# A 1 KB copy from input to output, issued on ScalarE's DMA ring at the start of a DMA-bound running logsumexp

## The chip, the cores and the metric

The kernel runs on one core of one Trainium2 chip. The metric is the device time of one execution in microseconds (us). Profiled runs also have a span, which is about 1.8 us shorter than the time.

## The reference, cut to what matters

```python
def setup_inputs():
    B, S, D = (4, 4096, 4128)
    return {'x': np.random.randn(B, S, D).astype(np.float32)}

def reference(x):
    ...
    out[:, 0, :] = x[:, 0, :].copy()
    for t in range(1, S):
        mx = np.maximum(out[:, t - 1, :], x[:, t, :])
        out[:, t, :] = mx + np.log(np.exp(out[:, t - 1, :] - mx) + np.exp(x[:, t, :] - mx))
```

It is a running logsumexp along S: 270.5 MB are read and 270.5 MB written, each once.

## The kernel before

The 4096 rows of each of four batches are cut into steps of 128 x 3 rows (and one of 128 x 2 per batch), 44 steps in all. A step is loaded into one of four buffers, goes through Exp (ScalarE), sums (VectorE, with TensorE for the sum over partitions) and Ln (ScalarE) in place, and is stored from the same buffer. SyncE issues every load and every store, in program order:

```python
    nc.scalar.preload_act_table_set("natural_log_exp_and_others")
    ...
        def load(self):
            full = xpool.tile([P, R, D], FP32, name="xt")
            self.xt = full[:, :self.r, :]
            nc.sync.dma_start(out=self.xt, in_=self.dram(x))

        def store(self):
            nc.sync.dma_start(out=self.dram(out), in_=self.xt)
    ...
    ahead = bufs - 1                 # bufs is 4
    for s in steps[:bufs]:
        s.load()
    stored = 0

    def result(k):
        nonlocal stored
        k.act(ACT.Ln)
        if k.c == lastc:
            k.t.store()
            if bufs <= stored + ahead < len(steps):
                steps[stored + ahead].load()
            stored += 1
```

The softmax here doesn't subtract the row's maximum and nothing guards it: scores larger than these inputs give would overflow.

Of the kernel before, what the change touches and what calls it, by code (L numbers as in the profile page):

```python
# [38 lines left out]
def kernel(  # L39
# [14 lines left out]
    nc = tc.nc  # L54
# [5 lines left out]
    order = [NC - 1] + list(range(NC - 1))  # L60
    firstc, lastc = order[0], order[-1]

    nc.scalar.preload_act_table_set("natural_log_exp_and_others")  # L63
    consts = ctx.enter_context(tc.tile_pool(name="consts", bufs=1))
    excl, rest, pick = _constants(nc, consts)
# [178 lines left out]
```

## Time and profile before

| | before |
|---|---|
| time, median of 6 runs | 1266.37 us (1263.28 to 1266.55) |
| span of the profiled run | 1262.5 us |
| ring of all loads and stores (q1) | 99.4% of 16 DMA engines' span |
| VectorE, ScalarE busy | 81%, 73% |
| HBM traffic | 270.53 MB read, 270.53 MB written |

The prediction shows the main lines: the sixteen DMA engines are full nearly throughout, so the bytes set the time. Two views of SyncE are added here, because the experiments turn on them. First its timeline of the first 70 us (columns: start, duration, engine, line, operation, tiles, count):

```profile
0.80 1.94 SPq L103 DMA_DIRECT2D xt<-in_x_dram  x4
41.31 22.79 SPq L106 DMA_DIRECT2D out_dram<-xt  x2
67.86 0.34 SPq L103 DMA_DIRECT2D xt<-in_x_dram  x1
```

The second row is two stores merged: one issued at 41.31 us, the other done being issued at 41.31 + 22.79 = 64.10 us. The fifth load follows at 67.86 us.

### The profile page before, as it was taken

How to read it: one execution, taken by the hardware profiler on the slowest of the kernel's cores; microseconds unless marked ns; L12 is line 12 of the kernel's file. 1: busy time of each engine (PE TensorE's matmuls, PEld its weight loads, DVE VectorE, ACT ScalarE, POOL GpSimd, SP SyncE). 2: the span in 40 equal slices, each digit the busy share in tenths (PEclk: the TensorE clock that was granted, in tenths of full speed). 3: DMA queues.
4: the chain of work that ended last, by engine and by line, in shares of the span. 5: the costliest groups of instructions: out<-in, count | busy, mean ns of one | idle time of the engine just before them, and what ended most of it. 6: DMA issues, size and time to landing. Idle time of an engine off the chain costs nothing.

```text
span 1262.5 us, 3545 instructions
## 1 busy us (share of the span) xinstructions
PE 480.5 (38%) x876; PEld 220.3 (17%) x876; DVE 1024.4 (81%) x858; ACT 921.0 (73%) x353; POOL 1.5 (0%) x10
## 2 busy tenths in 40 slices
PE   2445433333334434443324434443432443444332
PEld 1212111111111112211111112111111211111111
DVE  4999878888888888888679888887867988887784
ACT  4986677777777776668669776666966977666784
POOL 0000000000000000000000000000000000000000
PEclk9865555565555555556556565656555656555656
DMA  9999999999999999999999999999999999999997
GB/s 410 410 444 431 426 433 438 432 430 435 436 427 430 443 432 429 435 437 432 433 435 429 429 441 432 428 437 435 424 425 431 434 433 432 430 436 433 433 409 340
DMA packets 12692, 541.29 MB, mean 429 GB/s; under 512 B 1408, under 2 KB 1408, under 8 KB 1408
## 3 DMA queue, kind: packets, MB, share of 16 engines
q1 hardware_dynamic: 12672, 541.07, 99.4%
q8 instruction: 7, 0.11, 0.0%
q14 instruction: 13, 0.11, 0.0%
HBM read 270.53 MB, written 270.53 MB: 429 GB/s over the span
## 4 chain that ended last, share of the span: by engine, by line
DMA 69%; ACT 19%; issue 7%; DVE 3%; SPq 0%; PE 0%; DVEq 0%; ACTq 0%
DMA xt<-in_x_dram 63%; ACT xt L118 19%; DMA out_dram<-xt 6%; DVE xt L86 3%; DVE tot L86 1%; SPq L106 0%; PE above L83 0%; DVE carry L155 0%; DVEq L239 0%; ACTq L118 0%; DVE carry_t L155 0%; DVEq L86 0%
## 5 line engine op out<-in xcount | busy, mean ns | idle before, releaser
L118 ACT ACTIVATE xt<-xt 128x3072 f32<-128x3072 f32 (+3 forms) x352 | 919.7, 2692 | 328.8 <-DMA xt<-in_x_dram 315.0
L83 PE MATMUL above<-tot,excl 128*128 128x512 f32 (+1 forms) x396 | 255.1, 714 | 476.9 <-DVE tot L86 472.6
L86 DVE TENSOR_TENSOR xt<-xt,above 128x2048 f32<-128x2048 f32 (+3 forms) x220 | 393.4, 1788 | 0.0
L86 DVE TENSOR_TENSOR xt<-xt 128x1024 f32<-128x1024 f32 (+1 forms) x160 | 197.0, 1231 | 179.9 <-ACT xt L118 177.5
L86 DVE TENSOR_TENSOR tot<-xt 128x1024 fp32r<-128x1024 f32 (+1 forms) x176 | 217.1, 1234 | 40.4 <-ACT xt L118 18.9
L86 DVE TENSOR_TENSOR xt<-tot,above 128x1024 f32<-128x1024 f32 (+1 forms) x220 | 221.5, 1007 | 0.0
L83 PEld LDWEIGHTS above<-tot,excl 128*128 128x128 f32 x396 | 104.4, 305 | 607.4 <-DVE tot L86 566.9
L83 PE MATMUL above<-tot,rest 128*128 128x512 f32 x240 | 129.2, 633 | 205.1 <-DVE xt L86 205.1
L83 PE MATMUL above<-carry,pick 128*128 128x512 f32 x160 | 139.5, 972 | 0.0
L83 PEld LDWEIGHTS above<-tot,rest 128*128 128x128 f32 x240 | 53.1, 276 | 295.9 <-DVE xt L86 294.1
L83 PE MATMUL above<-carry_t,pick 128*128 128x32 f32 x80 | 25.2, 409 | 83.2 <-DVE xt L86 83.2
L83 PEld LDWEIGHTS above<-carry,pick 128*128 128x128 f32 x160 | 51.5, 322 | 11.1
L83 PEld LDWEIGHTS above<-carry_t,pick 128*128 128x128 f32 x80 | 20.2, 311 | 110.3 <-DVE xt L86 108.3
L155 DVE COPY carry<-xt 32x1024 f32<-32x1024 f32 x40 | 27.6, 691 | 1.4
L155 DVE COPY carry_t<-xt 32x32 f32<-32x32 f32 x40 | 7.1, 178 | 1.4
L63 ACT ACT_TABLE_LOAD x1 | 1.3, 1283 | 0.8 <-PEq L228 0.8
L77 DVE MEMSET carry<- 128x1024 f32 x1 | 0.9, 912 | 1.1 <-PEq L228 1.1
L24 POOL TENSOR_SCALAR_AFFINE_SELECT rest<-rest 128x128 fp32r<-128x128 f32 x1 | 0.3, 293 | 0.0
L24 POOL TENSOR_SCALAR_AFFINE_SELECT pick<-pick 128x128 f32<-128x128 f32 x1 | 0.3, 292 | 0.1
L24 POOL TENSOR_SCALAR_AFFINE_SELECT excl<-excl 128x128 fp32r<-128x128 f32 x1 | 0.3, 292 | 0.0
L23 POOL MEMSET excl<- 128x128 f32 x1 | 0.2, 204 | 0.3 <-POOLq L228 0.3
L23 POOL MEMSET rest<- 128x128 f32 x1 | 0.2, 204 | 0.0
(6 smaller groups left out, 0.7 us busy)
## 6 DMA issues: line engine op xcount, KB each, us to landing
xt<-in_x_dram SPq DMA_DIRECT2D x40, 6192.0 KB, 41.9
out_dram<-xt SPq DMA_DIRECT2D x40, 6192.0 KB, 27.7
xt<-in_x_dram SPq DMA_DIRECT2D x4, 4128.0 KB, 37.0
out_dram<-xt SPq DMA_DIRECT2D x4, 4128.0 KB, 25.4
```

Source lines behind the costliest of these rows:

```text
L23: nc.gpsimd.memset(t.bitcast(FP32), 1.0 - fill)
L24: nc.gpsimd.affine_select(out=t, in_=t, pattern=[[step, P]], compare_op=op, fill=fill, base=base, channel_multiplier=-step if step else 1,)
L63: nc.scalar.preload_act_table_set("natural_log_exp_and_others")
L77: nc.vector.memset(carry, 0.0)
L83: nc.tensor.matmul(o, lhsT=w, rhs=rhs, start=start, stop=True, skip_group_check=True)
L86: nc.vector.tensor_tensor(out=o, in0=a, in1=b, op=mybir.AluOpType.add)
L118: nc.scalar.activation(v, v, func)
L155: nc.vector.tensor_copy(cr[96:, :], t.xt[96:, n, a:b])
```

## The change

One line: before anything else, ScalarE copies 16 rows of 16 words from the input to the output. The rows are overwritten by the first store, so the result does not change. The likely intent is to see whether a second, otherwise unused ring costs or gives anything while the loads begin.

```diff
     firstc, lastc = order[0], order[-1]
 
+
+    nc.scalar.dma_start(out=out[0, :16, :16], in_=x[0, :16, :16])
     nc.scalar.preload_act_table_set("natural_log_exp_and_others")
```

The built programs differ by this one instruction on ScalarE, and by a wait: the first store waits for the copy as well.

## The prediction

> **What bounds the kernel now.** I read the page first: the busy shares, the slices, the DMA queues.
>
> ```profile
> PE 480.5 (38%) x876; PEld 220.3 (17%) x876; DVE 1024.4 (81%) x858; ACT 921.0 (73%) x353; POOL 1.5 (0%) x10
> ...
> DMA  9999999999999999999999999999999999999997
> ...
> q1 hardware_dynamic: 12672, 541.07, 99.4%
> q8 instruction: 7, 0.11, 0.0%
> q14 instruction: 13, 0.11, 0.0%
> ...
> xt<-in_x_dram SPq DMA_DIRECT2D x40, 6192.0 KB, 41.9
> out_dram<-xt SPq DMA_DIRECT2D x40, 6192.0 KB, 27.7
> ```
>
> No compute engine is above 81%, while the sixteen DMA engines are full in 39 of 40 slices. All 88 transfers go through one ring, q1, the one that SyncE issues on. Its packets fill 99.4% of the span of sixteen engines: 0.994 x 1262.5 = 1254.9 us for the mean engine. So only about 7.6 us of the span is not transfer. The packet records of the trace say the same from below: a row of three (49,536 bytes on one partition) has a median of 1829 ns and a row of two 1222 ns, and each engine carries 8 partitions of each of 80 large and 8 small transfers, 640 x 1.829 + 64 x 1.222 = 1248.8 us. Whatever keeps sizes and counts as they are cannot end much before that.
>
> Where the 7.6 us lie is read from the busy time by stretch (columns: stretch, length, busy us and count of each engine, granted clock, DMA share, GB/s):
>
> ```profile
> 0.00:15.00 15.00, 0.00 (x0) 0.00 (x0) 0.95 (x2) 3.17 (x3) 1.52 (x10) 1.00 0.94 387
> ...
> 60.00:120.00 60.00, 26.11 (x51) 12.39 (x51) 58.63 (x52) 51.72 (x20) 0.00 (x0) 0.59 1.00 432
> 120.00:240.00 120.00, 48.48 (x88) 22.48 (x88) 100.44 (x84) 86.00 (x32) 0.00 (x0) 0.56 1.00 432
> ...
> 600.00:1000.00 400.00, 148.25 (x273) 67.44 (x271) 322.12 (x272) 290.19 (x114) 0.00 (x0) 0.56 1.00 432
> ...
> 1220.00:1240.00 20.00, 7.65 (x16) 3.69 (x14) 14.40 (x14) 15.40 (x8) 0.00 (x0) 0.59 0.87 375
> 1240.00:1255.00 15.00, 4.52 (x8) 1.83 (x8) 8.47 (x8) 6.92 (x4) 0.00 (x0) 0.73 0.70 301
> ```
>
> The middle is full (share 1.00, 432 GB/s). What is lost lies at the start (0.06 x 15 = 0.9 us) and after 1220 us (0.13 x 20 + 0.30 x 15 = 7.1 us), where the last steps are computed with little left to load. The reader is to take two things from this: a delay of the first load moves the whole full stretch, so it comes out at the end one for one; and a delay on a compute engine early on costs nothing while the ring still has transfers queued.
>
> Last I read the timeline of the first 15 us and the waits, because the change sits there:
>
> ```profile
> 0.80 1.28 ACT L63 ACT_TABLE_LOAD   x1 [0.80 <-PEq L228]
> ...
> 0.80 1.94 SPq L103 DMA_DIRECT2D xt<-in_x_dram  x4
> ...
> 13.12 7.36 ACT L118 ACTIVATE xt<-xt 128x2112 f32<-128x2112 f32 x4 [11.04 <-DMA xt<-in_x_dram]
> ```
>
> SyncE issues four loads from 0.80 to 2.74 us, about 0.49 us each. ScalarE loads its table by 2.08 us and then stands idle for 11.04 us until the first load lands at 13.09 us. The first store is issued only at 41.31 us.
>
> **What the Trainium skill says.** (1) "DMA: Bandwidth & Descriptors", section "Issuing engines are not separate DMA queues": transfers begun by ScalarE and by SyncE end up on the same sixteen engines and interleave there; a second issuer saves only issue time. So the copy opens no further bandwidth. The trace before cannot confirm it, having one data ring. (2) The same page, "Queues, rings and completion order": an engine alternates between the rings that have work, at packet boundaries. Here a packet of the load lasts 1.2 us (step of two rows) or 1.8 us, so a copy that comes behind one waits at most about that long per engine; the trace shows a like case, instruction fetches (q8, q14) taken between the packets of q1. (3) The same page, "Specifications": below 512 bytes a write is a read-modify-write. The copy's rows are 64 bytes, so it is inefficient, but there are sixteen. (4) "ScalarE: Activation LUTs", "What ACT_TABLE_LOAD costs": about 1283 ns for the table load itself. The trace agrees to the digit (row of L63: 1 time, 1283 ns).
>
> **The change, part by part.** Removed: nothing. Moved: nothing; the comparison of instruction order shows ScalarE with one row more, a copy of 16x16 ahead of the table load, and the same rows on SyncE and GpSimd. On PE and VectorE only tile numbers differ. Each later transfer takes the next of the eight completion semaphores in rotation, the same rotation one place on, so no wait gets a new partner. One wait is new: the first store overwrites the rows the copy wrote, so it waits for the copy too.
>
> Issue on ScalarE: one issue like SyncE's, about 0.49 us (1.94 / 4), perhaps less with 16 rows for 128. The table load then ends at 2.08 + 0.49 = 2.6 us instead of 2.08; the first Exp starts at 13.12 on the landing. Slack 11.04 us, use 0.49: **cost 0**.
>
> New wait of the first store: the copy must have landed by 41.31 us. It is issued at about 0.8 us. Even behind a whole packet of the load on every engine (1.2 us) and with some us of latency (the first load's data begins to move about 1 us after its issue in the packet records, 1.8 us into the span), it is down before 6 us: **cost 0**.
>
> Bytes: 16 x 64 = 1 KB written and 1 KB read. At 429 GB/s that is 2.4 ns, beside 541 MB: **cost 0** as bandwidth. As packets it is one data packet more on each engine at most, where it now handles 704. The cost is thus a fixed time: an instruction fetch of 8 KB takes 0.31 us in mid-kernel in the packet records; I estimate 0.1 to 0.5 us for a read of 64 bytes and a small write, if nothing of it overlaps the load's packets.
>
> The first load's issue: both issuers start at about 0.80 us. If they share what generates descriptors, the load waits for the copy's issue, up to 0.49 us. I count half.
>
> Sum on the path: 0.25 (issue) + 0.25 (packets) + 0 + 0 = +0.5 us. Against 1266.3: **1266.8 us**, or +0.04%, which is less than the spread of the three runs before (1265.55 to 1266.43).
>
> **The rivals.**
> *A: the second ring costs something on every packet for the whole run*, because each engine now has two rings to look at. For it: nothing in this profile; q8 and q14 are further rings already in use, and the packets between their fetches stay at 1829 ns. Against it: an empty ring has nothing to move. For +2% (25 us) each of the 704 packets of an engine would need 36 ns more, so the median would be 1865 ns. A tenth of that gives 1269 us.
> *B: the first store waits long for the copy*, because the small writes starve behind four loads queued on the other ring, 23 MB, 53 us at 432 GB/s. Then the store moves from 41.31 to some 55 us, and a load waits for the buffer. But the loads queued behind it are what feeds the engines meanwhile, so perhaps 12 us would be lost, giving 1278. Turn-taking at packet boundaries speaks against it.
> *C: the start suffers more than I count*: the copy goes first on all engines and the load stands behind a full round trip to memory of 2 us. That makes 1268 us.
> *D: a second ring has a set-up or clean-up cost outside the span.* The profiled run took 1264.33 us for a span of 1262.5, so there is about 1.8 us outside. Half of it again would give 1267 to 1268.
> *E: faster.* The start and the tail hold 8 us of DMA idleness; the copy feeds neither. A chance shift of instruction fetches or of the skew between engines could move the end by about 1 us either way. Faster by 2% means 1241 us, below the 1248.8 us that the packets need at their present length: nearly excluded.
>
> **Range and chances.** The centre is 1266.8. Runs of one kernel agree within 0.07% here, yet another session may differ by some 0.2%, which is 2.5 us; C and D stretch the upper side to about 1270. So 1263.5 to 1270 at 8 in 10. Over 2% slower (beyond 1291.6) needs a strong form of A, or B with a restart: 0.04. Over 2% faster 0.02. Within 2%: 0.94.
>
> **What would show it.** Right: a new data queue with few packets and 0.0% share; q1 still 12672 packets at about 99.4%; the middle stretches still 1.00 and 432 GB/s; the first Exp at 13.1 to 13.6 us; the first store at 41.3 to 41.8 us; ScalarE's first wait still on the load. The issue step is wrong if the first load's issue begins more than 0.5 us later; the packet step, if the first landing moves by more than 1 us while the issue does not. Rival A shows as longer q1 packets or fewer than 430 GB/s in the middle, B as a wait of the first store on the copy, D as a time that grows while the span does not. The prediction fails outright if the full stretch, which the copy should never touch, runs at another rate.

## More of the kernel before

After the first store no load follows; the fifth load (step 4, into the buffer of step 0) stands behind the second store.

What it waited for is in SyncE's waits (total us, times, longest us):

```profile
SPq L103 <- DMA out_dram<-xt: 6.7, 5, 3.8
```

The longest of these, 3.8 us, is the fifth load waiting for the first store to land and free its buffer, from 64.10 to 67.86 us. So SyncE was ready for the fifth load 3.8 us before it could issue it. That bounds the slack at the start of this kernel.

## The result and the profile after

The changed kernel took 1265.8 us (median of 6 runs, 1264.71 to 1266.58), the kernel before 1266.37 us. The ratio is 1.0 with a 95% interval of 0.9987 to 1.0013: the same, to within 1.6 us. Ratios here are the mean time of one kernel's runs over that of the other's of the same rounds, so not quite the ratio of the medians quoted beside them. (Of the medians, the changed kernel has the smaller by 0.6 us; the profiled execution of it has the longer span by 1.9 us, 1264.4 for 1262.5. Neither is outside the spread of one kernel's runs, which for the kernel before is 3.3 us.)

The page after, its queues and the issue of the copy (queue, packets, MB, share; then KB and us from issue to landing):

```profile
q1 hardware_dynamic: 12672, 541.07, 99.3%
...
q10 hardware_dynamic: 32, 0.00, 0.0%
...
out_dram<-in_x_dram ACTq DMA_DIRECT2D x1, 1.0 KB, 7.4
```

A new ring, q10, carries 32 packets: one of 64 bytes and one for the semaphore on each engine. The ring of the loads has the same packets as before.

The timeline of the start after:

```profile
0.80 0.64 ACTq L64 DMA_DIRECT2D out_dram<-in_x_dram  x1
...
0.80 1.92 SPq L105 DMA_DIRECT2D xt<-in_x_dram  x4
...
1.47 1.28 ACT L65 ACT_TABLE_LOAD   x1 [1.47 <-PEq L230]
...
13.12 7.36 ACT L120 ACTIVATE xt<-xt 128x2112 f32<-128x2112 f32 x4 [10.37 <-DMA xt<-in_x_dram]
```

ScalarE and SyncE issue at the same time, and neither waits for the other: SyncE's four issues take 1.92 us where they took 1.94. The table load moves from 0.80 to 1.47 us, ScalarE's idle time shrinks from 11.04 to 10.37 us, and the first Exp starts at 13.12 us in both kernels.

The busy time by stretch after, in the columns of the prediction:

```profile
60.00:120.00 60.00, 27.32 (x51) 12.88 (x51) 58.63 (x52) 51.65 (x20) 0.00 (x0) 0.56 1.00 432
120.00:240.00 120.00, 47.36 (x88) 22.32 (x88) 100.45 (x84) 85.99 (x32) 0.00 (x0) 0.59 1.00 432
...
600.00:1000.00 400.00, 150.40 (x272) 68.34 (x272) 321.88 (x272) 289.89 (x114) 0.00 (x0) 0.55 1.00 431
```

The full stretch is as full as before and as fast, to 1 GB/s.

### The profile page after: what moved, and what is told of

Same layout as the page of the kernel before. It is cut to its first block, busy times and chain, and to the rows that moved or that the text cites. A ratio compares the mean times of both kernels' runs of the same rounds, so it can differ in the third digit from the quotient of the medians.

```text
span 1264.4 us, 3546 instructions
## 1 busy us (share of the span) xinstructions
PE 478.2 (38%) x876; PEld 220.0 (17%) x876; DVE 1024.3 (81%) x858; ACT 920.9 (73%) x353; POOL 1.5 (0%) x10
## 3 DMA queue, kind: packets, MB, share of 16 engines
q1 hardware_dynamic: 12672, 541.07, 99.3%
## 4 chain that ended last, share of the span: by engine, by line
DMA 69%; ACT 19%; issue 6%; DVE 3%; SPq 0%; PE 0%; DVEq 0%; ACTq 0%
DMA xt<-in_x_dram 63%; ACT xt L120 19%; DMA out_dram<-xt 6%; DVE xt L88 3%; DVE tot L88 1%; SPq L108 0%; PE above L85 0%; DVE carry L157 0%; DVEq L241 0%; ACTq L120 0%; DVE carry_t L157 0%; DVEq L88 0%
```

## The experiments

The theory: the change is free because ScalarE issues beside SyncE in time that it would spend waiting for the first load, because the copy's two packets (one of data, one for the semaphore) take 11 + 9 = 20 ns of each engine, and because the one wait on it ends long before it could matter. The rivals: a second ring slows the packets of the first (A), the first store is held up by the copy (B), and the start suffers more than counted (C). Since a cost of 1 us cannot be timed directly here, the experiments enlarge each suspect. Each time below is followed by that of the kernel before in the same rounds.

### e1: the same copy on SyncE, ahead of the loads

```diff
-    nc.scalar.dma_start(out=out[0, :16, :16], in_=x[0, :16, :16])
+    nc.sync.dma_start(out=out[0, :16, :16], in_=x[0, :16, :16])
```

> The same copy, but issued by SyncE ahead of the four loads, on the ring of the loads. My theory (the change is free because ScalarE issues at the same moment as SyncE and only 20 ns of packets per engine go in): here the issue stands before the first load, so the load's issue moves by about 0.5 to 0.65 us (1.44 instead of 0.80), the first landing from 13.09 to about 13.6, and the time by +0.5 us, within noise of 1266. Rival (an issue is free wherever it stands): first landing stays at 13.1.

Measured: 1265.66 us against 1265.45 (ratio 1.0004, 0.9989 to 1.0019). The timeline of SyncE:

```profile
0.80 0.63 SPq L64 DMA_DIRECT2D out_dram<-in_x_dram  x1
1.49 2.08 SPq L105 DMA_DIRECT2D xt<-in_x_dram  x4
```

The loads are issued at 1.49 instead of 0.80 us, and the first Exp starts at 13.95 us instead of 13.12, so the copy does cost the start 0.8 us when it stands ahead in SyncE's queue: 0.7 us of it is the later issue. That is a little more than the 0.5 us expected. On ScalarE it cost none. In the total, 0.8 us is below what three rounds resolve. The copy landed 2.0 us after its issue, on a ring with nothing ahead of it.

### e2: the same copy on SyncE, behind the four loads

```diff
-    nc.scalar.dma_start(out=out[0, :16, :16], in_=x[0, :16, :16])
 ...
     for s in steps[:bufs]:
         s.load()
+    nc.sync.dma_start(out=out[0, :16, :16], in_=x[0, :16, :16])
```

> The same copy issued by SyncE after the four loads, on the same ring. Then its packets stand behind 23 MB of loads, so it should land at about 57 to 59 us instead of 8.2, and the first store, which waits for it, moves from 41.3 us to there. This is rival B of the prediction made real. The ring runs dry for about one store issue plus latency, some 2 to 3 us: I expect 1268 to 1270. If the second ring did not matter, the landing would be at 8 us and the time unchanged.

Measured: 1267.35 us against 1265.45 (ratio 1.0018, 1.0001 to 1.0035). SyncE's waits, its first store, and the stretch from 31 to 60 us:

```profile
SPq L107 <- DMA out_dram<-in_x_dram: 53.7, 1, 53.7
```

```profile
57.16 6.88 SPq L107 DMA_DIRECT2D out_dram<-xt  x2
```

```profile
31.00:60.00 29.00, 11.84 (x24) 5.33 (x23) 28.34 (x24) 28.96 (x12) 0.00 (x0) 0.97 0.91 392
```

The same stretch in the kernel before:

```profile
31.00:60.00 29.00, 12.98 (x25) 5.77 (x23) 28.34 (x24) 29.00 (x12) 0.00 (x0) 0.93 0.98 409
```

Here rival B is real. The first store waits 53.7 us for 1 KB, is issued at 57.16 us instead of 41.31, and the DMA share of this stretch falls from 0.98 to 0.91, some 2 us. (This view counts a packet whole in the stretch in which it starts. The packet records, cut at the ends of the stretch, give 1.7 us: no engine moves data from 56.5 to 58.0 us.) The total grew by about that much: 0.18% of 1265 us is 2.3 us, though the interval runs from 0.1 to 4.4 us. So what spared the changed kernel this wait was that its copy had a ring of its own and overtook the loads.

### e3: a copy of 128 rows on ScalarE's ring

```diff
-    nc.scalar.dma_start(out=out[0, :16, :16], in_=x[0, :16, :16])
+    nc.scalar.dma_start(out=out[0, :128, :16], in_=x[0, :128, :16])
```

> A copy of 128 by 16 words on ScalarE's ring: 8 data packets and one semaphore packet on each engine instead of 1 and 1. Turn-taking packet by packet: each waits for one load packet of 1.22 us (later 1.83 us), so the copy lands at 16 to 19 us instead of 8.2, and the first load is late by no more than 8 x 11 ns = 0.1 us. Rival (a ring is drained once its turn comes): landing near 7.5 us. In both cases the time stays at 1266.

Measured, one look: 1265.62 us. The issue of the copy:

```profile
out_dram<-in_x_dram ACTq DMA_DIRECT2D x1, 8.0 KB, 16.1
```

It landed 16.1 us after its issue, at 16.9 us. In the packet records, the first packet of the copy starts at 6.21 us on the earliest engine, the next at 7.44, then 8.66, 9.89, 11.12: one load packet of 1.22 us between each two. The rings take turns packet by packet, and the first load loses no more than 0.1 us: the first Exp starts at 13.22 us.

### e4: 38 copies, one per step

```diff
-    nc.scalar.dma_start(out=out[0, :16, :16], in_=x[0, :16, :16])
 ...
+            if stored + 6 < len(steps):
+                f = steps[stored + 6]
+                blk = (f.b, slice(f.row, f.row + 16), slice(0, 16))
+                nc.scalar.dma_start(out=out[blk], in_=x[blk])
             stored += 1
```

> 38 copies of 16 by 16 words on ScalarE's ring, one at the end of each step, so that the second ring is used through the whole run. Theory (an issue costs idle ScalarE time, a copy 20 ns of each engine): 38 x 0.64 = 24 us of ScalarE's 329 us of idle time, 38 x 0.02 = 0.8 us of ring: 1266 to 1268. Rival A (a second ring in use slows each packet): middle stretches below 430 GB/s, q1 packets longer than 1829 ns, time above 1275. It also tells why the copy of the change waited three load packets before it moved: with packets already taken by the engine ahead of it, the landing comes 8 to 10 us after the issue here (packets of 1.83 us); with a fixed latency, 7.4 us; with a descriptor generator that was busy with SyncE's loads, 2 to 4 us.

Measured: 1264.89 us against 1265.45 (ratio 0.9998, 0.9983 to 1.0012). The queues, and a full stretch:

```profile
q1 hardware_dynamic: 12672, 541.07, 99.3%
q10 hardware_dynamic: 1216, 0.04, 0.1%
```

```profile
600.00:1000.00 400.00, 150.00 (x273) 68.69 (x273) 322.38 (x273) 290.44 (x113) 0.00 (x0) 0.56 1.00 433
```

With a copy on the second ring in 38 of the 44 steps, the first still moves 433 GB/s and its median packet of three rows still lasts 1829 ns. Rival A falls. The upper end of the interval, 0.12% or 1.5 us, divided by 38 gives at most 0.04 us for one copy. From issue to landing a copy took 6.2 to 8.7 us here, median 7.8, so neither a busy generator (2 to 4 us) nor exactly the queue of packets that I had assumed (8 to 10 us) fits. The third figure, a fixed latency (7.4 us), comes nearest, but the landings scatter by 2.5 us. e9 and e10 look further.

### e5: the first load later

```diff
+    back = cpool.tile([16, 16], FP32, name="back")
+    for _ in range(8):
+        nc.sync.dma_start(out=back, in_=x[0, :16, :16])
     for s in steps[:bufs]:
         s.load()
```

This edit and those of e6 and e7 are made to the kernel before, without the copy.

> No copy to the output; instead eight tiny loads of 16 by 16 words on SyncE ahead of the four loads, each waiting for the one before (one tiny transfer took 2.0 us from issue to landing on the idle ring in e1). The first real load is then issued about 7 x 2.1 + 0.7 = 15 us later. Theory (a delay of the first load comes out at the end one for one): the time grows by 15 us, to about 1281 us. Rival (the start has slack): less than half of it.

Measured: 1276.05 us against 1265.56 (ratio 1.008, 1.0065 to 1.0095). SyncE's timeline:

```profile
0.80 10.59 SPq L184 DMA_DIRECT2D back<-in_x_dram  x8
11.43 1.94 SPq L103 DMA_DIRECT2D xt<-in_x_dram  x4
```

I had overestimated a tiny load: the eight took 10.6 us, not 15. The first load is 11.43 - 0.80 = 10.6 us later, and the median 10.5 us: one for one, as the theory has it. The start of the ring has no slack.

### e6 and e7: ScalarE later

```diff
+    for _ in range(20):              # e7: 40
+        nc.scalar.activation(carry, carry, ACT.Copy)
     for s in steps[:bufs]:
         s.load()
```

> The kernel before with 20 copies of 128 by 1024 on ScalarE ahead of its first Exp, some 20 us, so that the first Exp starts at about 22 instead of 13.1 us and the first store is issued at about 50 instead of 41.3 us. The four loads fill the ring until about 57 us, so the theory (ScalarE's delay is free while the ring has work) says no change, 1266. Rival (ScalarE's time at the start is on the path): +9 us, 1275.

> The same with 40, some 40 us: first Exp at about 42, first store at about 70 us. The ring now runs dry from 57 to 70 us. Theory: +12 to +15 us, about 1279. If ScalarE had no part in the end, no change; if its whole delay counted, +29 us, 1295.

Measured: 1273.45 us for e6 and 1295.51 for e7, against 1265.56 (ratios 1.0063, 1.0048 to 1.0078, and 1.0239, 1.0224 to 1.0254). The first Exp starts at 23.71 us in e6 and 45.47 us in e7, 10.6 and 32.4 us later than before. Both expectations were wrong: e6 was to cost nothing, e7 12 to 15 us, and they cost 7.9 and 30 us. SyncE's timeline of e6 shows where, and the stretch from 60 to 120 us shows how much:

```profile
48.35 25.84 SPq L106 DMA_DIRECT2D out_dram<-xt  x2
74.25 0.42 SPq L103 DMA_DIRECT2D xt<-in_x_dram  x1
```

```profile
60.00:120.00 60.00, 28.19 (x54) 12.53 (x53) 58.76 (x48) 52.48 (x20) 0.00 (x0) 0.63 0.87 362
```

The first store is still in time; it lands at 67.7 us, as before. But the second store is issued only by 48.35 + 25.84 = 74.19 us, 10.1 us later than before, and the fifth load stands behind it in SyncE's order. So the ring has nothing: in the packet records no engine moves data from 67.35 us (0.4 us before the landing) to 74.69 us (0.5 us after the issue). On the mean engine this stretch has 0.13 x 60 = 7.8 us without transfers, which is the whole cost.

In e7 the first store is late too:

```profile
70.11 25.84 SPq L106 DMA_DIRECT2D out_dram<-xt  x2
```

Here the ring is empty twice, from 56.5 to 71.0 us and, until the second store is issued by 95.95 us, from 80.9 to 96.5 us; the expectation counted the first gap alone. Up to 200 us the mean engine has 30.5 us more without transfers than in the kernel before, against 30 measured. The second stores come 10.1 and 31.9 us late and the costs are 7.9 and 30 us, so about 2 us of the 3.8 us wait can be used. The rest goes to the time between the last packet and the landing, to that between an issue and its first packet, and to engines that finish at different times.

### e11: e6 with the fifth load ahead of the second store

This run tests the reading just given.

```diff
-            if bufs <= stored + ahead < len(steps):
+            if stored == 0:
+                steps[bufs].load()
+            if bufs < stored + ahead < len(steps):
                 steps[stored + ahead].load()
```

> e6 cost 8 us where I had expected none. The reading now: the fifth load stands behind the second store in SyncE's order, and in e6 that store was issued at 74.2 us while the first store had landed at 67.7, so the ring was empty for some 6.5 us. Here the same 20 copies delay ScalarE, but SyncE issues the fifth load right after the first store, ahead of the second. If the reading is right, the fifth load is issued at about 67.7 us, the ring stays full, and the time falls back to about 1266 to 1267. If ScalarE's own delay is what counts, it stays near 1273.5.

Measured: 1267.82 us against 1264.75 (ratio 1.0023, 1.0006 to 1.004). The timeline and the same stretch:

```profile
67.76 0.33 SPq L103 DMA_DIRECT2D xt<-in_x_dram  x1
```

```profile
60.00:120.00 60.00, 28.26 (x54) 12.60 (x52) 58.76 (x48) 53.14 (x20) 0.00 (x0) 0.65 0.96 402
```

The fifth load is back at 67.76 us, and the cost falls from 0.63% to 0.23%, so most of the 8 us was indeed SyncE's order. About 3 us remain (the interval runs from 0.8 to 5.1), more than expected. Part of it is seen: the fifth load cannot be issued before the first store lands, and the second store, which fills that moment in the kernel before, is still 6 us away, so no engine moves data from 67.4 to 68.7 us; this stretch has 1.8 us without transfers by the packet records (2.4 by the share above). The rest is not explained, and the new order without the 20 copies was not run.

### e8: the copy widened to 2.1 MB

```diff
-    nc.scalar.dma_start(out=out[0, :16, :16], in_=x[0, :16, :16])
+    nc.scalar.dma_start(out=out[0, :128, :], in_=x[0, :128, :])
```

> The copy of the change widened to 128 whole rows, 2.1 MB, on ScalarE's ring. Here the bytes must show: 8 packets of 16.5 KB on each engine at the rate of the loads (49,536 bytes in 1.829 us) are 8 x 0.61 = 4.9 us, all on the full ring, so the time grows by 4.9 us to about 1271. It also delays the first landing, because its packets take turns with those of the first load: about 13.1 + 3 x 0.6 = 15 us. Rival (a second ring adds bandwidth): no change in time.

Measured: 1269.97 us against 1265.56 (ratio 1.0031, 1.0015 to 1.0048), +4.4 us by the medians where 4.9 were worked out. The issue of the copy and the first Exp:

```profile
out_dram<-in_x_dram ACTq DMA_DIRECT2D x1, 2064.0 KB, 14.9
```

```profile
19.06 7.36 ACT L120 ACTIVATE xt<-xt 128x2112 f32<-128x2112 f32 x4 [16.32 <-DMA xt<-in_x_dram]
```

Bytes on the second ring are paid for at the rate of the first, within an interval of 1.9 to 6.1 us. My figures for the packets and the first landing were wrong. Each engine carried three packets of 44,032 bytes, 1.63 us each, not eight of 16.5 KB. All three went by before the first load was done, so the first Exp starts at 19.06 us instead of 13.12: 4.9 us of the delay are these packets, and the last 1.0 us is a wider spread between the engines (the first load's packets end between 17.2 and 18.7 us, in the changed kernel between 12.2 and 12.8).

### e9: the copy with the ring of the loads still empty

```diff
     nc.scalar.dma_start(out=out[0, :16, :16], in_=x[0, :16, :16])
 ...
+    back = cpool.tile([16, 16], FP32, name="back")
+    nc.sync.dma_start(out=back, in_=out[0, :16, :16])
     for s in steps[:bufs]:
         s.load()
```

> The copy of the change on ScalarE's ring, but SyncE first reads the copied words back into a small tile and therefore waits for the copy before it issues anything. So the copy runs with empty engines. If the 7.4 us from issue to landing in the changed kernel come from the load packets ahead of it, it lands about 2 us after its issue, as on SyncE's ring in e1; if ScalarE's ring or a copy from memory to memory is slow in itself, 7 us again. The time grows by the delay of the first load, some 3 us.

Measured, one look: 1266.73 us against 1267.02. The issues:

```profile
out_dram<-in_x_dram ACTq DMA_DIRECT2D x1, 1.0 KB, 1.9
```

1.9 us instead of 7.4: ScalarE's ring is not slow, and neither is a copy from memory to memory. The 5.5 us between are due to the traffic of the loads. (e9 also keeps SyncE from issuing at the same moment, but that is not needed for the wait: in e4 SyncE's next store was typically issued 6 us after the copy's issue, and the copy's data still took 3.3 us to move.) The first Exp started 2.5 us later (15.65 us); one run does not show that in the time.

### e10: packets of two rows throughout

```diff
-R = 3
+R = 2
```

This edit is to e4.

> As e4, but every step has two rows on a partition instead of three, so that the packets of the loads and stores are 33,024 bytes and 1.22 us long in the whole run. In e4 the copy's data moved 3.3 to 5.1 us after the end of its issue, the spread being one packet of 1.83 us. If a set number of packets (the running one and one more) goes ahead of it, the wait here is 2.6 to 3.9 us; if a set number of bytes (two packets of 33 KB for one of 49.5 KB), 3.9 to 5.1 us; a fixed latency beside the running packet gives 3.3 to 4.5 us. The time of this kernel is not compared.

Measured, one look: 1295.31 us, a slower kernel, not compared. Its 58 copies were read from the packet records. From the end of the issue to the first and the last of the 16 data packets it was typically 3.2 to 4.5 us, where e4 has 3.3 to 5.1. The lower end is the same with packets of 1.22 and of 1.83 us, and the spread is about one packet. So neither a set number of packets nor a set number of bytes goes ahead; a nearly constant 3.2 us and then the rest of the running packet fits both runs. One copy met an empty ring (its issue began at 54.23 us): its data moved 0.78 us after the end of the issue, and it landed 1.8 us after the issue began. So the constant part is some 2.4 us longer under load. In the changed kernel the data moved 4.7 to 5.2 us after the end of the issue; the engines still run nearly in step there, so up to 1.2 us of that can be the running packet, which still leaves 0.2 to 0.8 us. What makes up the 2.4 us is left open.

## Why the prediction was right, point by point

The time fell within the range, and within 2% as forecast. The centre, 1266.8 us, was 1.0 us above the median, and the predicted sign of +0.5 us can be neither confirmed nor denied at 1.6 us of resolution. Both terms that made up the 0.5 us turned out to be nearly nothing; that they were wrong does not show, because they were small.

- **The bound.** Right. The ring's 12672 packets, their share and the 432 GB/s of the full stretch stayed, so the time stayed. A delay of the first load comes out one for one: 10.6 us gave 10.5 (e5). Where the ring is idle was misread, without effect on the sum: 0.06 x 15 = 0.9 us at the start comes from the view that counts a packet whole where it starts. In the packet records the first 15 us lose 2.0 us (the first data moves at 1.8 us), and the time after 1210 us loses 7.4.
- **Issue on ScalarE.** Right in kind: cost 0, since the first Exp starts at 13.12 us in both. The size was 0.64 us rather than 0.49.
- **The first load's issue, counted at 0.25 us.** This term of the sum was 0: SyncE's issues began at 0.80 us and took 1.92 us, with ScalarE issuing beside them. Behind the copy in the same queue they do start 0.69 us later (e1).
- **Packets, counted at 0.25 us.** The term measured 0.02 us: 11 ns for the 64 bytes and 9 ns for the semaphore, per engine. The estimate of one data packet left out the semaphore's. No run shows the read-modify-write that the prediction named for rows under 512 bytes.
- **The new wait of the first store.** Right in the result, wrong on the way. The copy landed at 8.2 us, not before 6, because it did not wait "at most about" one packet: three packets of the load went ahead of it on each engine (1.8 to 6.1 us) and one more ahead of its semaphore packet. The turn-taking that the Trainium skill states holds once both rings have their packets at the engine (e3); what it does not give is the 3 to 5 us that a new transfer takes to get there while the engines are full (e4, e10). The 33 us left until the first store covered the error.
- **Rival A** fell in e4, where it had 38 chances. **Rival B** does not happen in the changed kernel; it does when the copy shares the ring of the loads (e2), and then it costs 2 us, not the 12 I gave it, since the first store's data has to stand behind the same loads anyway. **Rival C**: nothing to see in the changed kernel, whose first landing stayed; even with the copy ahead of the loads (e1) the start lost 0.8 us, not 2. **Rival D**: time minus span is 1266.16 - 1264.4 = 1.8 us in the profiled run, as before. **Rival E**: no gain shows, and the gap of 0.6 us between the medians is noise.
- **The general remark** that a delay on a compute engine early on costs nothing while the ring has transfers queued was read too generously in e6 and e7. The ring stays full only if the next issue comes in time, and SyncE's order left a wait of 3.8 us, of which about 2 can be used once ScalarE starts later than the first landing. The change delayed ScalarE by 0.67 us, all of it before the first landing.

## What to carry to other kernels

A small transfer on an otherwise idle ring of another issuer was free here, because that issuer was waiting anyway, while the same transfer in the queue of the big loads delayed what stood behind it or waited behind them. To say how much delay a start can bear, do not take the idle time of the compute engine alone, but find the first wait of the issuing queue that ends on a transfer. Its length bounds the slack (3.8 us here, about 2 usable), and the order of loads and stores in that queue decides it. Where a change is too small to time, multiply it (38 copies here) or enlarge it until it shows.

## What the Trainium skill lacked or had wrong

- "DMA: Bandwidth & Descriptors", "Queues, rings and completion order": turn-taking by packet agrees (e3: one packet of the copy per load packet of 1.22 us). A packet of the loads was here a whole partition's 33,024 or 49,536 bytes, 1.22 or 1.83 us long, which sets the pace of the other ring; the section gives a packet's size in descriptors.
- The same page, "Latency and other measured facts", gives about 600 ns to the first byte for such an issuer. An empty ring comes near it if one counts from the end of the issue (0.78 us, e10; from its start 1.3 us); with full engines it was 3.2 us and then the rest of the running packet (e4, e10). The section has 0.2 us on average and 2 us at high load for an access to HBM, which could be 1.8 of these 2.4 us; no run here separates it.
- The same page, "Issuing engines are not separate DMA queues", says that a second issuer saves only issue time. For bandwidth this agrees (e8: 2.1 MB cost 4.4 us). But it also saves a small transfer from waiting behind large ones: it landed 7.4 us after its issue on ScalarE's ring and 54.3 us on SyncE's behind the loads (e2). That follows from the turn-taking in the other section, but this one does not say it.
- No page that I read says so: the first copy that a ring carried took 0.61 to 0.65 us to issue, whichever engine issued it, and most later ones 0.52 us (e1, e4, e10).
